# Placing matmul operands at different offsets modulo 256 bytes in SBUF, in a two-layer hybrid block kernel

## Chip, cores and metric

One core of a Trainium2 chip. The metric is the device time of one execution in microseconds; lower is better. All times stand for the whole program, from inputs in HBM to the output in HBM.

## What is computed

The reference runs two layers over 512 tokens of width 1024, all in float32:

```python
h = rms_norm(x, g_pre_mix)
proj = h @ w_in                                  # q, k, v, qi, ki, wi, xr, gr, zu, zv, gates
y_a = dsa_attention(q, k, v, qi, ki, wi)         # indexer picks 128 keys, then attention
y_b = rg_lru(conv(xr)) * gelu(gr)
y_c = chunked_spatial_gating(gelu(zu), rms_norm(gelu(zv)))
merged = einsum(sigmoid(gates), [y_a, y_b, y_c] @ w_branch)
x = x + rms_norm(merged @ w_out, g_post_mix)
f = square(relu(rms_norm(x) @ w_ffn_up)) @ w_ffn_down
x = x + rms_norm(f, g_post_ffn)
x = x + rms_norm((p @ w_ple) * sigmoid(x @ w_ple_gate), g_post_ple)
```

## The kernel before

Activations lie transposed: 128 features on the partitions, the 512 tokens along the free dimension, so one tile is 128 x 512 floats, 2 KB in each partition. A float32 product is made of three fast products (`mm3`, L296 to L299): every operand is split into a high part, rounded to the chip's `fp32r` type, and a low part, what is left; the matmuls are high by high, low weights by high activations, high weights by low activations. So TensorE gets three matmuls with 512 columns for each 128 x 128 block of weights, and each of them has weights of its own to load.

The names of the operands are those of the trace. `wr` is a weight tile as it comes by DMA (128 x 1024 floats, three buffers), `wh` and `wl` its two parts (four buffers each); `prep` (L231) issues the transfer on SyncE's queue, makes `wh` on ScalarE (L242) and `wl` on VectorE (L243), and `getw` (L246) keeps this three tiles ahead. `xh0` to `xh7` and `xl0` to `xl7` are the two parts of the normed activations ("the parts of x", `XS`, L470); they stream in the input projections, in the up projection of the feed-forward part and in its gate. `K0`, `K1`, `V0`, `V1` are 8 KB tiles that serve in turn as keys, values, merged activations and as the hidden activations of the even quarters of the feed-forward part (`K` the high parts, `V` the low ones); `A0` to `A7` (high) and `B0` to `B7` (low) hold the hidden activations of the odd quarters (L1064 to L1069), and before that queries, branch inputs and temporaries. In `ps<-xh,wl` the streamed operand stands first and the loaded one second.

The order of the work is written out by hand: `gemm` (L301) runs the blocks of one weight tile, 24 matmuls, into one of eight PSUM banks; `gemm_arriving` (L334, matmuls at L355) does the first four output tiles of a stage block by block while the activations are still being made; `gemm_halves` (L321) does the last three tiles of a stage in token halves of 256 columns. `tokens` (L578, L589) swaps the operands, so that x is loaded and weights stream. A planner with a clock of its own (`tick`, L285) puts indexer, attention and recurrence between these matmuls when the program is built; it knows no address.

Where a tile lies comes from the order in which the tags of a pool are first asked for: the pools `cp`, `wp`, `tp` and `ep` follow each other, and in each the tags follow each other with their buffers. In the kernel before, `lead` (L122) ends at a multiple of 256 bytes. All tiles after it are 2 KB, 4 KB or 8 KB, so each of x's parts, `K`, `V`, `A`, `B`, `M`, `R`, `wr`, `wh`, `wl` and `tmp` begins at a multiple of 256 bytes in its partition. Slices of them that are loaded or streamed are 512, 1024 or 2048 bytes apart, so every matmul of `mm3` has both operands at the same place modulo 256.

```python
76      def slot(tag, dt=F32, big=False):
77          return cp.tile([128, 4, S] if big else [128, S], dt, tag=tag, name=nm(tag))
...
122     cp.tile([128, LEAD // 4], F32, tag="lead", name="lead")
123     X = [cp.tile([128, S], F32, tag=f"X{k}", name=f"X{k}") for k in range(KT)]
...
240         hi = wp.tile([128, 1024], F32R, tag="wh", name=nm("wh"), bufs=NWB)
241         lo = wp.tile([128, 1024], F32R, tag="wl", name=nm("wl"), bufs=NWB)
242         A.copy(hi, raw)
243         V.tensor_sub(lo, raw, f32v(hi))
...
296     def mm3(ps, wh, wl, xh, xl, start, stop):
297         PE.matmul(ps, wh, xh, start=start, stop=False)
298         PE.matmul(ps, wl, xh, start=False, stop=False)
299         PE.matmul(ps, wh, xl, start=False, stop=stop)
...
470     XS = [(slot(f"xh{k}", F32R), slot(f"xl{k}", F32R)) for k in range(KT)]
```

Of the kernel before, what the change touches and what calls it, by code (L numbers as in the profile page):

```python
# [8 lines left out]
F32 = mybir.dt.float32  # L9
F32R = mybir.dt.float32r  # L10
# [40 lines left out]
def hybrid_block_kernel(ctx, tc, xT, pT, pos, vec, bsp, freq, w_in, w_tok, w_lru, w_sp, w_br, w_out, w_up, w_dn, w_ple, w_gate, out, depth=DEPTH, dbg=None):  # L51
    nc = tc.nc
    V, A, G, PE = nc.vector, nc.scalar, nc.gpsimd, nc.tensor

    cp = ctx.enter_context(tc.tile_pool(name="cp", bufs=1))
# [7 lines left out]
    def nm(p):  # L63
        uid[0] += 1
        return f"{p}_{uid[0]}"

    def tmp(dt=F32):
        return tp.tile([128, S], dt, tag="tmp", name=nm("tmp"), bufs=NTMP)
# [4 lines left out]
    def bank():  # L73
        return pp.tile([128, 512], F32, tag="ps", name=nm("ps"), bufs=8)

    def slot(tag, dt=F32, big=False):
        return cp.tile([128, 4, S] if big else [128, S], dt, tag=tag, name=nm(tag))
# [168 lines left out]
    def getw(key, ahead=LA):  # L246
        assert order[nget[0]][0] == key, (order[nget[0]][0], key)
        nget[0] += 1
        while nprep[0] < min(nget[0] + ahead, len(order)):
            prep()  # L250
        return prepared.pop(key)
# [49 lines left out]
    def gemm(ps, w, xs, kk, c0=0, st=None, r=FULL):  # L301

        h3, l3 = [v.rearrange("p (k c) -> p k c", k=kk) for v in w]
        for k in range(kk):
            if st is not None and k == kk - 2:
                st.partial()
            mm3(ps, h3[:, k, c0:c0 + 128], l3[:, k, c0:c0 + 128], xs[k][0][:, r], xs[k][1][:, r], k == 0, k == kk - 1)
            tick(0.65 * width(r) / S)
# [12 lines left out]
    def gemm_halves(keys, xs, evac, done):  # L321


        ws = [getw(key, LA if i == 0 else 0) for i, key in enumerate(keys)]
        for r in HALVES:
            for i, w in enumerate(ws):
                ps = bank()[:, :S // 2]
                gemm(ps, w, xs, KT, r=r)
                evac(i, r, ps)
                if r is HALVES[1] and nprep[0] < len(order):  # L330
                    prep()
            done(r)

    def gemm_arriving(keys, xs, source, ranges, arrived=None, lag=LAG, tail=TAIL):  # L334


        n = len(keys)
        ws = [getw(key, 0) for key in keys[:-1]]
        pss = [bank() for _ in keys]
        last = {}  # L340
        for r in ranges:
            gen = source(r)
            for k in range(KT):
                with ordered(last):
                    next(gen)
                    todo = [(o, k) for o in range(len(ws))]
                    if len(ws) < n and k == lag:
                        ws.append(getw(keys[-1], 0))
                        todo += [(n - 1, q) for q in range(k + 1)]
                    if r is ranges[-1] and k >= KT - tail:  # L350
                        todo = [] if k < KT - 1 else [(o, q) for o in range(n) for q in range(KT - tail, KT)]
                    for i, (o, q) in enumerate(todo):
                        h3, l3 = [v.rearrange("p (k c) -> p k c", k=KT) for v in ws[o]]
                        for m in range(3):
                            PE.matmul(pss[o][:, r], (h3, l3, h3)[m][:, q], xs[q][m // 2][:, r], start=q == 0 and m == 0, stop=q == KT - 1 and m == 2)  # L355
                        if r is ranges[-1] and q == KT - 1 and o < n - 1:
                            prep()
                tick(0.65 * len(todo) * width(r) / S)
            if arrived is not None:
                arrived(r)  # L360
        while nprep[0] < nget[0] + LA:
            prep()
        return pss
# [84 lines left out]
    class Norm:  # L448
# [16 lines left out]
        def source(self, r):  # L465
            while r.start not in self.gens:
                tick(0.1)
            return self.gens[r.start]

    XS = [(slot(f"xh{k}", F32R), slot(f"xl{k}", F32R)) for k in range(KT)]  # L470

    def x_tiles(r, xs, g=None, st=None, ys=None, bc=None, gp=None, on_g=()):

        def updated(d):
            if ys is not None and d < KT:
                if gp is None:
                    V.tensor_mul(ys[d][:, r], ys[d][:, r], bc)
                else:  # L480
                    V.scalar_tensor_tensor(ys[d][:, r], ys[d][:, r], gp[:, d:d + 1], bc, op0=ALU.mult, op1=ALU.mult)
                (G if d in on_g else V).tensor_add(X[d][:, r], X[d][:, r], ys[d][:, r])  # L482

        updated(0)
        for d in range(KT):
            x = X[d][:, r]
            if xs is not None:
                hi, lo = [v[:, r] for v in xs[d]]
                if g is None:
                    A.copy(hi, x)  # L490
                else:
                    A.activation(hi, x, AF.Copy, scale=g[:, d:d + 1])  # L492
                if st is not None:
                    st.square(x, r)
            updated(d + 1)
            if st is not None:
                st.accumulate(r)
            if xs is not None:
                if g is None:
                    V.tensor_sub(lo, x, f32v(hi))  # L500
                else:
                    V.scalar_tensor_tensor(lo, x, g[:, d:d + 1], f32v(hi), op0=ALU.mult, op1=ALU.subtract)  # L502
            yield d
# [28 lines left out]
    for l in range(depth):  # L532
# [6 lines left out]
        if l == 0:  # L539
            st = Stats()  # L540

            def gen():
                tiles = x_tiles(FULL, XS, vc[:, V_PRE:V_PRE + 8], st)
                for k in range(KT):
                    first_parts(k)
                    yield next(tiles)
# [5 lines left out]
        rt = st.rt  # L552
        first = gemm_arriving([("in", l, f"xr{j}") for j in range(3)], XS, norm.source if l else lambda r: gen0, HALVES if l else (FULL,), st.row(D, R), 0, TAIL if l else 1)

        def proj(name, ahead=LA):
            ps = bank()
            gemm(ps, getw(("in", l, name), ahead), XS, KT)
            return ps
# [11 lines left out]
        def rope(ps, n=128):  # L570
            t1, u = tmp(), tmp()
            V.tensor_mul(t1[:n], ps[:n], Cr[:n])
            V.stream_shuffle(u[:n], ps[:n], mask=SHUF)
            G.tensor_mul(u[:n], u[:n], Sr[:n])  # L574
            G.tensor_add(t1[:n], t1[:n], u[:n])  # L575
            return t1

        def tokens(n, fn):  # L578
# [3 lines left out]
            for t0 in (0, 2):  # L582
                pss = [bank(), bank()]
                for k in range(KT):
                    wh, wl = [v[:, k % 2] for v in ws[k // 2]]
                    for t, ps in enumerate(pss, t0):
                        xh, xl = [v[:, t * 128:(t + 1) * 128] for v in XS[k]]
                        for i, (x, w) in enumerate(((xh, wh), (xl, wh), (xh, wl))):
# [247 lines left out]
        for j in range(4):  # L836
# [7 lines left out]
            r, i = tmp(), tmp()  # L844
# [165 lines left out]
        for j in range(4):  # L1010
            f = rope(proj(f"q{j}"))
# [31 lines left out]
        def out_evac(d, r, ps):  # L1043
            st.add(ps, r)
            A.activation(Y[d][:, r], ps, AF.Copy, scale=col(V_POST + d))

        for d in range(5):
            ps = bank()
            gemm(ps, getw(("out", l, d)), M, KT)
            out_evac(d, FULL, ps)  # L1050
        norm = Norm(st, D, lambda r, bc: x_tiles(r, XS, vc[:, V_FFN:V_FFN + 8], st2, Y, bc, on_g=(1, 3, 5)))
        gemm_halves([("out", l, d) for d in (5, 6, 7)], M, lambda i, r, ps: out_evac(5 + i, r, ps), norm.complete)


        R = cp.tile([128, S], F32, tag="R", name=nm("R"))
        first = gemm_arriving([("up", l, 0, i) for i in range(4)], XS, norm.source, HALVES, st2.row(D, R))
        ps = bank()
# [172 lines left out]
```

## Time and profile before

| | |
|---|---|
| time, median of 3 runs | 1858.88 us (1858.13 to 1859.21) |
| the profiled execution: its own time | 1859.11 us |
| the profiled execution: its span | 1857.4 us |
| granted TensorE clock, mean | 0.99 of full speed |
| TensorE busy with matmuls | 1804.0 us (97%) |
| VectorE / ScalarE / GpSimd busy | 63% / 43% / 19% |
| read from HBM | 164 MB, 90 GB/s |

The span runs from the first to the last instruction of the profiled execution; its own time lies a little above it, and close to the median. PE is TensorE's matmul side, PEld its loading of weights, DVE VectorE, ACT ScalarE, POOL GpSimd, SPq the queue on which SyncE issues transfers. Matmuls are pipelined: the duration of one in the trace is longer than the distance from its start to the start of the next, and it is the distance that adds up.

### The profile page before, as it was taken

What the parts mean: (1) busy time and instruction counts of PE and PEld (TensorE: products, weight loads), DVE (VectorE), ACT (ScalarE), POOL (GpSimd) and SP (SyncE); (2) the same over time, 40 slices, a digit from 0 to 9 for tenths busy, and PEclk for the clock granted to TensorE, in tenths of its full rate; (3) what the DMA queues carried; (4) which work ended last, traced back from release to release, by engine and by line L of the source; (5) the groups of instructions that cost most, each with busy time, mean ns of one, the idle gap of its engine ahead of it and who ended that gap; (6) DMA issues with size and microseconds to landing.
All of it is one profiled execution on the core that took longest, in us unless ns stands there. A gap on an engine that the chain in (4) does not pass through costs nothing.

```text
span 1857.4 us, 22874 instructions
## 1 busy us (share of the span) xinstructions
PE 1804.0 (97%) x8798; PEld 1507.9 (81%) x8798; DVE 1161.0 (63%) x1939; ACT 800.9 (43%) x1292; POOL 361.3 (19%) x292
## 2 busy tenths in 40 slices
PE   8899999999999999999998999999999999999997
PEld 7787777888888888888887877877888888888886
DVE  6689986666386253533685999866563852545355
ACT  5466435564353231323554572455544432222233
POOL 3513212210140000003354141222003200000033
PEclk9999999999999999999999999999999999999998
DMA  5122222222223222232212122221222222222321
GB/s 172 63 91 90 87 97 84 76 78 82 80 91 103 100 93 102 91 114 91 89 60 97 66 93 92 102 80 69 91 80 91 91 91 102 92 101 94 111 80 58
DMA packets 49678, 167.77 MB, mean 90 GB/s; under 512 B 6048, under 2 KB 8864, under 8 KB 49568
## 3 DMA queue, kind: packets, MB, share of 16 engines
q1 hardware_dynamic: 47376, 163.64, 25.7%
q10 hardware_dynamic: 2192, 2.67, 0.4%
q8 instruction: 69, 1.13, 0.2%
q14 instruction: 41, 0.34, 0.1%
HBM read 164.19 MB, written 2.10 MB: 90 GB/s over the span
## 4 chain that ended last, share of the span: by engine, by line
PE 72%; DVE 14%; POOL 5%; issue 4%; ACT 4%; DMA 0%; SPq 0%; POOLq 0%; DVEq 0%; ACTq 0%
PE ps L297 20%; PE ps L299 20%; PE ps L298 20%; PE ps L589 4%; PE ps L355 4%; DVE wl L243 2%; DVE tmp L706 2%; DVE m L704 2%; POOL tmp L574 1%; POOL tmp L575 1%; PE ps L958 1%; POOL sacc L397 1%; POOL X L482 1%; PE ps L671 1%; DVE tmp L781 1%
## 5 line engine op out<-in xcount | busy, mean ns | idle before, releaser
L242 ACT CAST wh<-wr 128x1024 fp32r<-128x1024 f32 x303 | 316.7, 1049 | 453.2 <-PE ps L299 369.2
L243 DVE TENSOR_TENSOR wl<-wr,wh 128x1024 fp32r<-128x1024 f32 x303 | 386.0, 1278 | 190.7 <-ACT wh L242 189.9
L297 PE MATMUL ps<-xh,wh 128*128 128x512 f32 (+1 forms) x1296 | 502.2, 388 | 0.0
L298 PE MATMUL ps<-xh,wl 128*128 128x512 f32 (+1 forms) x1296 | 495.1, 382 | 3.0 <-DVE wl L243 3.0
L299 PE MATMUL ps<-xl,wh 128*128 128x512 f32 (+1 forms) x1296 | 495.4, 382 | 0.0
L397 POOL TENSOR_TENSOR sacc<-sacc,tmp 128x256 f32<-128x256 f32 (+1 forms) x99 | 109.7, 1109 | 893.7 <-issue 584.5
L299 PEld LDWEIGHTS ps<-xl,wh 128*128 128x128 f32 x1296 | 243.7, 188 | 48.2
L298 PEld LDWEIGHTS ps<-xh,wl 128*128 128x128 f32 x1296 | 244.0, 188 | 46.9 <-DVE wl L243 3.8
L297 PEld LDWEIGHTS ps<-xh,wh 128*128 128x128 f32 x1296 | 243.8, 188 | 45.5 <-issue 1.9
L299 PE MATMUL ps<-V,wh 128*128 128x512 f32 (+1 forms) x528 | 195.5, 370 | 0.0
L297 PE MATMUL ps<-K,wh 128*128 128x512 f32 (+1 forms) x432 | 158.2, 366 | 0.0
L298 PE MATMUL ps<-K,wl 128*128 128x512 f32 (+1 forms) x432 | 157.9, 365 | 0.0
L299 PE MATMUL ps<-B,wh 128*128 128x512 f32 x336 | 131.0, 390 | 0.0
L297 PE MATMUL ps<-A,wh 128*128 128x512 f32 x320 | 125.0, 391 | 0.0
L298 PE MATMUL ps<-A,wl 128*128 128x512 f32 x320 | 124.6, 389 | 0.0
L1089 DVE TENSOR_TENSOR M<-M,ps 128x512 f32<-128x512 f32 x48 | 33.0, 688 | 141.4 <-PE ps L299 141.4
L299 PEld LDWEIGHTS ps<-V,wh 128*128 128x128 f32 x528 | 99.5, 188 | 16.8
L1077 DVE TENSOR_TENSOR tmp<-ps,R 128x512 f32<-128x512 f32 x64 | 43.9, 691 | 108.4 <-PE ps L299 108.4
L355 PE MATMUL ps<-xl,wh 128*128 128x256 f32 (+1 forms) x264 | 88.2, 334 | 7.7 <-DVE xl L502 6.9
L297 PEld LDWEIGHTS ps<-K,wh 128*128 128x128 f32 x432 | 81.5, 189 | 13.2
L298 PEld LDWEIGHTS ps<-K,wl 128*128 128x128 f32 x432 | 81.5, 189 | 13.1
L355 PE MATMUL ps<-xh,wh 128*128 128x256 f32 (+1 forms) x264 | 86.5, 328 | 1.0 <-ACT xh L492 1.0
(237 smaller groups left out, 2738.5 us busy)
## 6 DMA issues: line engine op xcount, KB each, us to landing
wr<-in_w_in_dram SPq DMA_DIRECT2D x95, 512.0 KB, 3.2
wr<-in_w_up_dram SPq DMA_DIRECT2D x64, 512.0 KB, 3.2
wr<-in_w_dn_dram SPq DMA_DIRECT2D x64, 512.0 KB, 3.2
wr<-in_w_br_dram SPq DMA_DIRECT2D x24, 512.0 KB, 3.2
wr<-in_w_tok_dram SPq DMA_DIRECT2D x16, 512.0 KB, 3.2
wr<-in_w_out_dram SPq DMA_DIRECT2D x16, 512.0 KB, 3.2
wr<-in_w_gate_dram SPq DMA_DIRECT2D x16, 512.0 KB, 3.2
X<-in_xT_dram SPq DMA_DIRECT2D x8, 256.0 KB, 5.2
```

What stands on the lines that cost most here:

```text
L242: A.copy(hi, raw)
L243: V.tensor_sub(lo, raw, f32v(hi))
L297: PE.matmul(ps, wh, xh, start=start, stop=False)
L298: PE.matmul(ps, wl, xh, start=False, stop=False)
L299: PE.matmul(ps, wh, xl, start=False, stop=stop)
L355: PE.matmul(pss[o][:, r], (h3, l3, h3)[m][:, q], xs[q][m // 2][:, r], start=q == 0 and m == 0, stop=q == KT - 1 and m == 2)
L397: G.tensor_add(sacc[:, r], sacc[:, r], self.q[r.start, r.stop])
L589: PE.matmul(ps, x, w, start=k == 0 and i == 0, stop=k == KT - 1 and i == 2)
L704: V.max(m8, (sc if r == 0 else wk)[:, :n])
L706: V.match_replace(wk[:, :n], m8, (sc if r == 0 else wk)[:, :n], -3.0e38)
L1077: V.tensor_mul(t, ps, R)
L1089: V.tensor_add(F[d], F[d], ps)
```

## The change

Four filler tiles are put into the pool `cp`, ahead of the parts of x, between x and `K`/`V`, between these and `A`/`B`, and after them. So that the groups lie in that order, `K`, `V`, `A` and `B` are asked for once at this point, ahead of their first use. The fillers are 32, 32, 32 and 224 bytes in each partition. Modulo 256 the parts of x then begin at 32, `K` and `V` at 64, `A` and `B` at 96, and all that follows, `R`, `M`, `wr`, `wh`, `wl` and `tmp`, at 64 (320 bytes in all). X itself, the rope tables and `sacc` stay where they were. Nothing else is changed.

```diff
@@ -467,7 +467,23 @@
                 tick(0.1)
             return self.gens[r.start]
 
+
+    GAPS = (32, 32, 32, 224)
+
+    def gap(i):
+        if GAPS[i]:
+            cp.tile([128, GAPS[i] // 4], F32, tag=f"gap{i}", name=f"gap{i}")
+
+    gap(0)
     XS = [(slot(f"xh{k}", F32R), slot(f"xl{k}", F32R)) for k in range(KT)]
+    gap(1)
+    for n in ("K0", "K1", "V0", "V1"):
+        slot(n, F32R, True)
+    gap(2)
+    for n in range(8):
+        slot(f"A{n}", F32R)
+        slot(f"B{n}", F32R)
+    gap(3)
 
     def x_tiles(r, xs, g=None, st=None, ys=None, bc=None, gp=None, on_g=()):
```

## Rows read from the trace of the kernel before

**Rows 1.** The page: busy time by engine, and the chain that ended last.

```profile
PE 1804.0 (97%) x8798; PEld 1507.9 (81%) x8798; DVE 1161.0 (63%) x1939; ACT 800.9 (43%) x1292; POOL 361.3 (19%) x292
...
PE 72%; DVE 14%; POOL 5%; issue 4%; ACT 4%; DMA 0%; SPq 0%; POOLq 0%; DVEq 0%; ACTq 0%
PE ps L297 20%; PE ps L299 20%; PE ps L298 20%; PE ps L589 4%; PE ps L355 4%; DVE wl L243 2%; DVE tmp L706 2%; DVE m L704 2%; POOL tmp L574 1%; POOL tmp L575 1%; PE ps L958 1%; POOL sacc L397 1%; POOL X L482 1%; PE ps L671 1%; DVE tmp L781 1%
```

**Rows 2.** Timeline, PE, ends of three runs of 192 matmuls: start us, us, what.

```profile
606.75 0.39 PE L297 MATMUL ps<-K,wh 128*128 128x512 f32 x1
...
650.04 0.39 PE L299 MATMUL ps<-V,wh 128*128 128x512 f32 x1
650.27 0.39 PE L297 MATMUL ps<-xh,wh 128*128 128x512 f32 x1
...
693.56 0.39 PE L299 MATMUL ps<-xl,wh 128*128 128x512 f32 x1
693.79 0.39 PE L297 MATMUL ps<-A,wh 128*128 128x512 f32 x1
...
737.08 0.39 PE L299 MATMUL ps<-B,wh 128*128 128x512 f32 x1
```

**Rows 3.** Groups of the page and by form: xcount | busy us, mean ns | idle.

```profile
L297 PE MATMUL ps<-xh,wh 128*128 128x512 f32 (+1 forms) x1296 | 502.2, 388 | 0.0
...
L355 PE MATMUL ps<-xh,wh 128*128 128x256 f32 (+1 forms) x264 | 86.5, 328 | 1.0 <-ACT xh L492 1.0
...
L299 PE MATMUL ps<-B,wh 128*128 128x512 f32 x336 | 131.0, 390 | 0.0
...
L298 PE MATMUL ps<-A,wl 128*128 128x512 f32 x320 | 124.6, 389 | 0.0
...
L298 PE MATMUL ps<-B,wl 128*128 128x512 f32 x80 | 31.3, 391 | 0.0
...
L299 PE MATMUL ps<-A,wh 128*128 128x512 f32 x64 | 24.9, 389 | 0.0
```

**Rows 4.** Stretches at either clock (PEclk the share granted), and steps in the first.

```profile
999.43:1002.40 2.97, 2.97 (x8) 2.31 (x7) 2.94 (x5) 0.00 (x0) 1.00 (x1) 0.50 0.54 185
606.75:650.05 43.30, 43.30 (x193) 35.86 (x192) 11.70 (x11) 12.41 (x16) 0.00 (x0) 1.00 0.28 95
...
999.86 0.63 PE L589 MATMUL ps<-wh,xh 128*128 128x512 f32 x1
...
1001.14 0.63 PE L589 MATMUL ps<-wh,xh 128*128 128x512 f32 x1
```

**Rows 5.** Timeline, PE and PEld: a matmul, the next weights' load, the next matmul.

```profile
691.07 0.39 PE L297 MATMUL ps<-xh,wh 128*128 128x512 f32 x1
691.07 0.19 PEld L298 LDWEIGHTS ps<-xh,wl 128*128 128x128 f32 x1
...
691.30 0.39 PE L298 MATMUL ps<-xh,wl 128*128 128x512 f32 x1
```

**Rows 6.** The page: weight transfers (count, KB, us to landing), and VectorE's share of preparing.

```profile
L243 DVE TENSOR_TENSOR wl<-wr,wh 128x1024 fp32r<-128x1024 f32 x303 | 386.0, 1278 | 190.7 <-ACT wh L242 189.9
...
wr<-in_w_up_dram SPq DMA_DIRECT2D x64, 512.0 KB, 3.2
```

**Rows 7.** Groups by form, VectorE: two streams from SBUF, and one from PSUM.

```profile
L369 DVE TENSOR_TENSOR B<-tmp,A 128x512 fp32r<-128x512 f32 x32 | 21.9, 684 | 0.0
...
L369 DVE TENSOR_TENSOR tmp<-ps,tmp 128x512 fp32r<-128x512 f32 x16 | 11.0, 689 | 7.1 <-ACT tmp L368 4.6 <-POOL tmp L575 2.4
```

**Rows 8.** Timeline, PE, after an interruption: ends of nine steps.

```profile
544.14 0.40 PE L298 MATMUL ps<-xh,wl 128*128 128x512 f32 x1
...
546.22 0.39 PE L298 MATMUL ps<-xh,wl 128*128 128x512 f32 x1
```

**Rows 9.** Timeline, PE, 256 columns: ends of four steps and of 22 steps.

```profile
516.18 0.28 PE L355 MATMUL ps<-xh,wh 128*128 128x256 f32 x1
...
516.65 0.28 PE L355 MATMUL ps<-xh,wl 128*128 128x256 f32 x1
...
532.84 0.28 PE L355 MATMUL ps<-xh,wl 128*128 128x256 f32 x1
...
535.48 0.28 PE L355 MATMUL ps<-xl,wh 128*128 128x256 f32 x1
```

## Prediction

> **What bounds the kernel now.** I read the page first: TensorE is busy for 1804.0 of 1857.4 us and holds 72% of the chain that ended last, the three matmuls of `mm3` (L297 to L299) 20% each; VectorE follows with 14% [rows 1]. So the time is mostly the number of matmuls times the distance from the start of one to the start of the next. That distance comes from the timeline, over three unbroken runs of 192 matmuls of 512 columns (first and last row of each): with K and V streaming, 606.75 to 650.04; with the parts of x, 650.27 to 693.56; with A and B, 693.79 to 737.08 [rows 2]. Each is 43.29 us over 191 steps, 226.6 ns. The reader is to see that it is the same to the rounding in all three, and that in all three both operands lie at the same place modulo 256: the kernel before has no run that differs in the one thing that the change alters. How many matmuls are concerned comes from the groups: x streams in 3 groups of 1296 (L297 to L299) and 3 of 264 (L355), 4680; A and B stream in one group of 336, two of 320, two of 80 and one of 64, 1200 [rows 3]. Together 5880.
>
> What a matmul could cost is seen where the granted clock is at its lower level. At 999.43 to 1002.40 it is 0.50 (1.2 GHz); three steps take 1001.14 - 999.86 = 1.28 us, 426.7 ns each, and the window 606.75 to 650.05 has 1.00 (2.4 GHz) [rows 4]. Half of 426.7 is 213.3. So at full clock each matmul pays 226.6 - 213.3 = 13.3 ns over its columns, and at half clock nothing. The load of the next weights starts together with the matmul (both at 691.07) and ends at 691.26, before the next matmul at 691.30 [rows 5]: two reads run side by side through the first half of every matmul. A cost that is there at full rate and gone at half rate is what two colliding reads would look like; it is also what a fixed step that half rate hides would look like. That is the whole question.
>
> **The change, part by part.** (1) Four filler tiles: no instruction, no transfer; 320 bytes a partition. They cost nothing. (2) K, V, A and B are asked for once more, early: this settles only where they lie; no instruction, no wait, no queue is moved. (3) K, V, M, R, the weight buffers, `tmp`: all 64 bytes further. Weights against K and V stay at difference 0, so I leave those matmuls at 226.6 ns. (4) The weight transfers now land 64 bytes past a multiple of 256. The trace has no such landing. Now they take 3.2 us [rows 6], and a tile's 24 matmuls take 24 x 226.6 ns = 5.4 us, with three raw buffers ahead: half as long again would still hide behind the matmuls, so the sum takes 0; without that cover each late tile would cost the excess directly. (5) VectorE and ScalarE read and write at the new places. Two streams out of SBUF, `B<-tmp,A`, both at multiples of 256, take 684 ns for 512 columns; with one stream from PSUM, `tmp<-ps,tmp`, 689 ns [rows 7]. Equal places do not slow VectorE, so there is nothing to win or lose there: 0, within 5 ns a piece. (6) What is left: 4680 matmuls with x 32 bytes ahead of the weights, and 1200 with A or B 32 bytes behind.
>
> The price of (6) is not in the trace; it has to be bounded. Best end: the 13.3 ns go altogether, 5880 x 13.3 = 78 us, 1781. Worst end: after an interruption the steps stay long for a while, 544.14 to 546.22 for nine steps, 231.1 ns, 4.5 ns above the steady value [rows 8]; all 5880 at that level is 26 us, 1885. That the steps are longer there, with the same tiles at the same places, speaks for a cost that depends on how the two reads lie against each other. There are steps below the steady value as well: with 256 columns, 516.18 to 516.65 is four steps in 0.47 us (117 ns at most after the rounding of 0.01), where 532.84 to 535.48 is 22 steps at exactly 120.0 [rows 9]: 3 ns less. A shift of 32 bytes is 8 columns, 3.3 ns of the stream at 213.3 / 512 ns a column: a step of the same size as the differences in timing under which these steps vary.
>
> I take 2 ns less for each of the 5880, two thirds of the 3 ns that the rows show, because x and A/B are moved in opposite directions and the same effect need not help both. 5880 x 2 = 11.8 us. TensorE is idle for only 53 of 1857 us [rows 1], so nearly all of it reaches the end; after it the weight preparation still fits (1.28 us on VectorE for the 5.4 us of matmuls of a tile [rows 6]), so nothing new becomes late. The profiled execution took 1859.1 us (span 1857.4 and 1.7 around it), 0.2 over the median of 1858.9: 1859.1 - 11.8 = 1847.3, against the median **1847**.
>
> A rule that speaks against all this: the Trainium skill, page "TensorE: Matmul & The Clock Gate", section "Part 2: What happens when you issue a matmul", says that loading the next weights and streaming the present operand use two independent read ports and that the one takes no bandwidth from the other. By that the sum is 0 and the time stays at 1858.9. The same page's formula in "Back-to-back issue gap" gives, as an estimate for 512 columns, 215.8 ns; the trace here has 226.6, so something costs 10.8 ns more than the page knows, and the rule leaves it open what.
>
> **The rivals.** *No dependence on the place.* The 13.3 ns are a fixed step between two matmuls with weights of their own. For it: the same 226.6 in all three runs, the same 13.3 at 256 columns (120.0 - 106.7), VectorE's indifference to places, and that two streams of different pace pass each other as often wherever they start. Against it: the steps that vary between 117 and 120, and between 226.6 and 231. Time: 1858.9. The rule of the skill named above ends here too.
>
> *The shift makes x worse.* The load begins within 0.01 us of its matmul. If it begins about 3.3 ns behind, x, now 32 bytes (3.3 ns) behind the weights' place, stands exactly at that place when the load starts, and both read the same lines at once; A and B move away from it. Then 4680 matmuls go to 231.1 ns, +4.5 x 4680 = 21 us, and A/B win 2 x 1200 = 2.4: 1858.9 + 18.7 = 1877.5. For it: x is four fifths of the affected matmuls, so its sign decides; with a 3.7 us bound, 0.8 ns more per x matmul is enough. Against it: at 10 ns resolution the lead of the matmul is not seen, and the long steps of rows 8 come after interruptions only and die out.
>
> *The whole excess goes* (the best end above): 1781 if complete for both, 1797 for x alone. Against it: no step of 512 columns in the rows is anywhere near 213.3.
>
> **How the numbers follow.** A difference under 0.2% (3.7 us) can't be told from no change here. Shorter steps for x and A/B, little or much: 0.46, mostly near 1847, with a tail to the best end; no dependence: 0.30; x worse: 0.24. The range runs from 1805 (9 ns of the 13.3 gone) to 1885 (all 5880 at the long level); about 0.05 lies below and 0.08 above. The likeliest case's own range is 1805 to 1855. Faster by over 0.2%: 0.46, within: 0.30, slower: 0.24.
>
> **What would show it.** The three runs of rows 2, timed again: x and A/B near 224.6 ns and K/V at 226.6 bears the forecast out; all three at 226.6 is the first rival; x near 231 and A/B below 226.6 the second. At half clock the step must stay 426.7 whatever happens. The landing of a weight tile should stay near 3.2 us, VectorE's and ScalarE's means as they are. The forecast is wrong if the time moves while the x runs keep 226.6 (then it came from waits, not from reads), or if K/V, whose difference is unchanged, moves as much as x.

## The result, and the profile after

The changed kernel takes 1878.67 us in the median of four runs (1875.80 to 1880.23) against 1858.51 of before: a ratio of 1.0107, interval 1.0089 to 1.0124. It is 20 us slower. The profiled execution is the 1875.80 one.

The page of the changed kernel: span, busy time by engine, the chain by engine, and the landing of a weight tile.

```profile
span 1874.1 us, 22874 instructions
...
PE 1829.7 (98%) x8798; PEld 1503.3 (80%) x8798; DVE 1160.8 (62%) x1939; ACT 801.7 (43%) x1292; POOL 362.4 (19%) x292
...
PE 72%; DVE 14%; POOL 5%; ACT 4%; issue 4%; DMA 0%; SPq 0%; POOLq 0%; ACTq 0%; DVEq 0%
...
wr<-in_w_up_dram SPq DMA_DIRECT2D x64, 512.0 KB, 3.3
```

Against [rows 1] the instructions are the same in number, VectorE, ScalarE and GpSimd do the same work to within 1.1 us each, and the chain is shared out in the same way. Only TensorE has grown, by 25.7 us, while the span grew by 16.7: its idle time fell from 53.4 to 44.4 us.

The timeline of the changed kernel, PE, at the ends of the three runs of 192 matmuls (start us, us, what):

```profile
606.55 0.39 PE L297 MATMUL ps<-K,wh 128*128 128x512 f32 x1
...
649.87 0.39 PE L299 MATMUL ps<-V,wh 128*128 128x512 f32 x1
650.10 0.40 PE L297 MATMUL ps<-xh,wh 128*128 128x512 f32 x1
...
694.66 0.40 PE L299 MATMUL ps<-xl,wh 128*128 128x512 f32 x1
694.90 0.40 PE L297 MATMUL ps<-A,wh 128*128 128x512 f32 x1
...
739.46 0.39 PE L299 MATMUL ps<-B,wh 128*128 128x512 f32 x1
```

These answer to [rows 2]. K/V, whose difference to the weights is still 0: 43.32 us over 191 steps, 226.8 ns, 0.03 us in all over before. x: 44.56 us, 233.3 ns. A/B: 44.56 us, 233.3 ns. Both shifts cost 6.7 ns a matmul, ahead or behind alike. From the first row to the last it takes 132.91 us where [rows 2] have 130.33: 2.58 us more, and 384 matmuls by 6.7 ns are 2.57. In this stretch the loss reaches the time one to one.

Two more stretches of the changed kernel's timeline, PE: 92 steps of 256 columns with x streaming, and three steps at half clock, with the window that shows the clock (the last column but two).

```profile
914.14 0.28 PE L297 MATMUL ps<-xh,wh 128*128 128x256 f32 x1
...
925.02 0.28 PE L299 MATMUL ps<-xl,wh 128*128 128x256 f32 x1
```

```profile
1003.30:1009.90 6.60, 5.69 (x13) 4.46 (x14) 4.67 (x7) 1.38 (x2) 2.78 (x2) 0.50 0.53 149
...
1004.80 0.63 PE L605 MATMUL ps<-wh,xh 128*128 128x512 f32 x1
...
1006.08 0.63 PE L605 MATMUL ps<-wh,xh 128*128 128x512 f32 x1
```

With 256 columns the shift helps: 10.88 us over 92 steps, 118.3 ns, where [rows 9] have 120.0. And at half clock it does nothing: 1.28 us for three steps, as in [rows 4].

In `tokens` the weights stream and x is loaded, so there, too, the two now lie 32 bytes apart. The ends of one run of 26 of its matmuls, before and in the changed kernel:

```profile
230.04 0.39 PE L589 MATMUL ps<-wh,xh 128*128 128x512 f32 x1
235.71 0.39 PE L589 MATMUL ps<-wh,xl 128*128 128x512 f32 x1
...
228.59 0.39 PE L605 MATMUL ps<-wh,xh 128*128 128x512 f32 x1
234.42 0.40 PE L605 MATMUL ps<-wh,xl 128*128 128x512 f32 x1
```

5.67 us over 25 steps against 5.83: 226.8 ns and 233.2. These matmuls lose as much as the others.

Who waited for whom (us in total, times, longest), entries of PE on the preparation of weights and of x, before and in the changed kernel:

```profile
PE ps L589 <- DVE wl L243: 16.3, 6, 4.2
PE ps L355 <- DVE xl L502: 6.9, 8, 3.7
PE ps L298 <- DVE wl L243: 6.3, 4, 1.6
...
PE ps L605 <- DVE wl L243: 14.0, 6, 4.2
PE ps L355 <- DVE xl L518: 6.1, 10, 2.5
PE ps L298 <- DVE wl L243: 3.1, 4, 1.2
```

TensorE waits most for these preparations on VectorE. When its matmuls get longer, the waits get shorter (for `wl` 17.1 us instead of 22.6), and that part of the loss never reaches the end.

### The profile page after: what moved, and what is told of

It reads as the page before. It is cut to its first block, busy times and chain, and to the rows that moved or that the text cites. A ratio compares the mean times of both kernels' runs of the same rounds, so it can differ in the third digit from the quotient of the medians.

```text
span 1874.1 us, 22874 instructions
## 1 busy us (share of the span) xinstructions
PE 1829.7 (98%) x8798; PEld 1503.3 (80%) x8798; DVE 1160.8 (62%) x1939; ACT 801.7 (43%) x1292; POOL 362.4 (19%) x292
## 4 chain that ended last, share of the span: by engine, by line
PE 72%; DVE 14%; POOL 5%; ACT 4%; issue 4%; DMA 0%; SPq 0%; POOLq 0%; ACTq 0%; DVEq 0%
PE ps L297 20%; PE ps L299 20%; PE ps L298 20%; PE ps L605 4%; PE ps L355 4%; DVE wl L243 2%; DVE tmp L722 2%; DVE m L720 2%; POOL tmp L590 1%; POOL tmp L591 1%; PE ps L974 1%; POOL sacc L397 1%; POOL X L498 1%; PE ps L687 1%; DVE tmp L797 1%
## 5 line engine op out<-in xcount | busy, mean ns | idle before, releaser
L297 PE MATMUL ps<-xh,wh 128*128 128x512 f32 (+1 forms) x1296 | 508.1, 392 | 0.0
L298 PE MATMUL ps<-xh,wl 128*128 128x512 f32 (+1 forms) x1296 | 501.6, 387 | 0.7 <-DVE wl L243 0.7
L299 PE MATMUL ps<-xl,wh 128*128 128x512 f32 (+1 forms) x1296 | 501.4, 387 | 0.0
L298 PEld LDWEIGHTS ps<-K,wl 128*128 128x128 f32 x432 | 81.5, 189 | 13.3
```

## The experiments

The question: what makes a step 233.3 ns instead of 226.7? The place of each operand by itself, the difference between the two, or something else that the new order of tiles brings along? Unless a diff says otherwise, a kernel here is the changed one with other fillers. All steps below are worked out as above, from the first and the last row of the runs of 192 matmuls.

**All at 32 past a multiple of 256.**

```diff
-    GAPS = (32, 32, 32, 224)
+    GAPS = (32, 0, 0, 0)
```

> One filler of 32 bytes ahead of the parts of x and none after it: x, K, V, A, B and the weights all begin at 32 modulo 256, so the difference between streamed and loaded operand is 0 everywhere. If the difference decides: the runs of 192 matmuls with x, K/V and A/B all step in 226.7 ns, and the time is that of before, 1858.5 us within 4. If what decides is that an operand does not begin at a multiple of 64 bytes: all three runs step in 233.3 ns, K/V too, and the time is some 1880 to 1890.

1859.34 us against 1859.40, ratio 1.000, interval 0.9990 to 1.0009. x and A/B in its timeline:

```profile
647.67 0.39 PE L297 MATMUL ps<-xh,wh 128*128 128x512 f32 x1
...
690.96 0.39 PE L299 MATMUL ps<-xl,wh 128*128 128x512 f32 x1
691.19 0.39 PE L297 MATMUL ps<-A,wh 128*128 128x512 f32 x1
...
734.48 0.39 PE L299 MATMUL ps<-B,wh 128*128 128x512 f32 x1
```

43.29 us over 191 steps each, 226.6 ns. The new order of the tiles, the early asking for K, V, A and B, and starting off a multiple of 64 cost nothing. With the differences back at 0, the whole loss is gone.

**x alone, A and B alone.**

```diff
-    GAPS = (32, 32, 32, 224)
+    GAPS = (0, 32, 0, 0)
```

> One filler of 32 bytes after the parts of x: x at 0, all else at 32 modulo 256. Only x differs from the weights, by 32 bytes ahead. If the difference decides: x steps in 233.3 ns, K/V and A/B in 226.7, and x's four fifths of the loss come back alone: 1858.5 plus 16, about 1874. If absolute places off a multiple of 64 decide: x (at 0) 226.7, K/V and A/B (at 32) 233.3, and a time of 1862 to 1870.

1870.45 us against 1859.40, ratio 1.0059, interval 1.0044 to 1.0074. The three runs:

```profile
607.10 0.40 PE L297 MATMUL ps<-K,wh 128*128 128x512 f32 x1
...
650.40 0.39 PE L299 MATMUL ps<-V,wh 128*128 128x512 f32 x1
650.63 0.40 PE L297 MATMUL ps<-xh,wh 128*128 128x512 f32 x1
...
695.19 0.40 PE L299 MATMUL ps<-xl,wh 128*128 128x512 f32 x1
695.43 0.39 PE L297 MATMUL ps<-A,wh 128*128 128x512 f32 x1
...
738.75 0.39 PE L299 MATMUL ps<-B,wh 128*128 128x512 f32 x1
```

x, the only one that stands at 0, is the slow one: 233.3 ns, while K/V and A/B at 32 take 226.7 and 226.8. The difference decides. Of the 16 us that were expected from x alone, 11 came.

```diff
-    GAPS = (32, 32, 32, 224)
+    GAPS = (0, 0, 32, 224)
```

> Fillers of 32 bytes ahead of A/B and 224 after them: A and B at 32, all else at 0. Both theories expect 233.3 ns in the A/B runs and 226.7 in the x and K/V runs; 1200 matmuls by 6.7 ns are 8 us at most, so 1862 to 1867. If the losses of x alone and of A/B alone do not add up to the 20 us of the change, the two are not independent.

1865.91 us against 1859.40, ratio 1.0033, interval 1.0022 to 1.0043; A/B 233.4 ns, x and K/V 226.6. The two parts add up to 17.6 us, the change to 20.2; by their intervals the parts make 12 to 22. They are independent as far as this can be told.

**Larger differences.** In the first kernel x lies 64 ahead of the weights, K/V 64 behind, A/B 128 behind; in the second x 96 ahead, K/V 96 behind, A/B level; in the third K/V lie 256 behind and A/B 288.

```diff
-    GAPS = (32, 32, 32, 224)
+    GAPS = (0, 128, 64, 128)
```

> Fillers 0, 128, 64, 128: x at 0, K/V at 128, A/B at 192, weights at 64 modulo 256. Every operand is at a multiple of 64 bytes; x lies 64 ahead of the weights, K/V 64 behind, A/B 128 behind. If absolute places off a multiple of 64 decide: 226.7 ns in all three runs and 1858.5 us. If the difference decides: at least one of the three leaves 226.7; a collision of the two reads that is worst at a distance of 32 and gone at a large one would give steps below 226.7 somewhere, down to 216; one in which 0 is the best place gives 227 to 240 in all three.

1877.09 us against 1859.40, ratio 1.0096, interval 1.0081 to 1.0111. Its three runs:

```profile
609.38 0.39 PE L297 MATMUL ps<-K,wh 128*128 128x512 f32 x1
...
653.09 0.39 PE L299 MATMUL ps<-V,wh 128*128 128x512 f32 x1
653.33 0.39 PE L297 MATMUL ps<-xh,wh 128*128 128x512 f32 x1
...
697.88 0.39 PE L299 MATMUL ps<-xl,wh 128*128 128x512 f32 x1
698.11 0.39 PE L297 MATMUL ps<-A,wh 128*128 128x512 f32 x1
...
742.50 0.39 PE L299 MATMUL ps<-B,wh 128*128 128x512 f32 x1
```

228.8 ns for K/V, 233.2 for x, 232.4 for A/B: all longer than at 0, none shorter, though every operand stands at a multiple of 64.

```diff
-    GAPS = (32, 32, 32, 224)
+    GAPS = (0, 192, 160, 0)
```

> Fillers 0, 192, 160, 0: x 96 bytes ahead of the weights, K/V 96 behind, A/B and the weights at the same place (96 past a multiple of 256). By the theory that the difference decides and 0 is the best place: A/B 226.7 ns, x and K/V between 228 and 236. By a theory of two reads that collide when near: x and K/V at or below 226.7, as far apart as they are. Time 1862 to 1885 by the first, under 1862 by the second.

1880.9 us (one run; before beside it 1859.4). x 234.2 ns, K/V 233.4, A/B 226.7: as expected if 0 is the best place, and not if it is nearness that costs.

```diff
-    GAPS = (32, 32, 32, 224)
+    GAPS = (0, 256, 32, 224)
```

> Fillers 0, 256, 32, 224: x and weights at 0 modulo 512, K/V 256 behind them modulo 512, A/B 288 behind. If the pattern repeats every 256 bytes: K/V 226.7 ns and A/B 233.3, as at 0 and at 32 behind. If its period is 512 or more: K/V leaves 226.7, or A/B leaves 233.3. x 226.7 either way. Time near 1866 by the first.

1864.1 us (one run; before beside it 1859.4). K/V and A/B:

```profile
604.71 0.39 PE L297 MATMUL ps<-K,wh 128*128 128x512 f32 x1
...
648.01 0.39 PE L299 MATMUL ps<-V,wh 128*128 128x512 f32 x1
...
691.75 0.40 PE L297 MATMUL ps<-A,wh 128*128 128x512 f32 x1
...
736.32 0.40 PE L299 MATMUL ps<-B,wh 128*128 128x512 f32 x1
```

226.7 ns at 256 as at 0, 233.4 at 288 as at 32: at these two places the pattern repeats after 256 bytes.

**Differences below 32.** The parts of x are slices of one tile here, begun 16, 4 and 8 bytes in (made from the kernel before, all else at 0):

```diff
-    XS = [(slot(f"xh{k}", F32R), slot(f"xl{k}", F32R)) for k in range(KT)]
+    XT = cp.tile([128, 2 * KT * S + 8], F32R, tag="xs", name="xs")
+    XP = [XT[:, 4 + i * S:4 + (i + 1) * S] for i in range(2 * KT)]
+    XS = [(XP[2 * k], XP[2 * k + 1]) for k in range(KT)]
+    cp.tile([128, 56], F32, tag="gap", name="gap")
```

> The parts of x in one tile, begun 16 bytes in, so that x lies at 16 modulo 256 and all else at 0: x 16 bytes behind the weights. If what matters is being in the same 32-byte piece: 226.7 ns in the x runs and 1858.5 us. If any difference counts, down to pieces of 16 bytes or less: x steps in 229 to 236 ns and the time is 1864 to 1876.

> The same with x begun one float (4 bytes) in: x 4 bytes behind the weights. If whole pieces of 16 or 32 bytes are read: the x runs keep about 226.7 ns unless a read off a multiple of 16 bytes costs something of its own. If the difference counts to the byte: 229 to 236 ns, as at 32.

> x in one tile begun two floats (8 bytes) in. At 16 bytes the x runs stepped in 231.6 ns, at 4 bytes in 238.3. If being off a multiple of 16 bytes adds a cost of its own, 8 bytes is near 238; if only being off a multiple of 8 does, near 231.6. If 226.7 is to be beaten at a small difference at all, it would have to show here.

16 bytes (4 floats, as in the diff): 231.6 ns and 1865.7 us. 4 bytes (1 in place of the 4): 238.3 ns and 1888.3 us. 8 bytes (2 in place of the first 4; the slices are then two columns longer than what is used): 233.3 ns and 1872.5 us. Each is one run, with before at 1857.7, 1857.7 and a median of 1858.3. Being in the same piece of 16 or 32 bytes does not help; one float off is the worst of all:

```profile
658.09 0.40 PE L297 MATMUL ps<-xs,wh 128*128 128x512 f32 x1
...
703.60 0.40 PE L299 MATMUL ps<-xs,wh 128*128 128x512 f32 x1
```

At 4 bytes the step lies above the 229 to 236 ns that were expected, and at 8 bytes it is near neither 238 nor 231.6. In these three kernels x alone, of the operands of `mm3`, stands off a multiple of 32 bytes, so whether its place costs something of its own, beside the difference, is not separated. No run has x in one tile begun at 0, so it is the steps that count here, and not the times.

The third column is from runs of 93 matmuls with 256 columns (92 steps) in the same traces.

| streamed less loaded operand, bytes modulo 256 | step at 512 columns, ns | step at 256 columns, ns | from |
|---|---|---|---|
| -96 | 234.2 | 117.3 | x, second kernel of the larger differences |
| -64 | 233.2 | 117.8 | x, first of them |
| -32 | 233.3 | 118.3 | x, the change |
| **0** | **226.6 to 226.8** | 119.9 | before; all at 32; K/V of the change; 256 |
| 4, 8, 16 | 238.3, 233.3, 231.6 | 123.0, 119.9, 113.5 | x in one tile |
| 32 | 233.3 | no run | A/B, the change |
| 64 | 228.8 | 117.8 | K/V, first of the larger differences |
| 96 | 233.4 | 119.9 | K/V, second of them |
| 128 | 232.4 | no run | A/B, first of them |

With 512 columns, 0 is the best of the differences tried, and no kernel here is faster than the one before by more than the noise. With 256 columns it is not: there the lowest step is the one at 16 bytes. Its run, and the same run before:

```profile
910.78 0.28 PE L297 MATMUL ps<-xs,wh 128*128 128x256 f32 x1
921.22 0.28 PE L299 MATMUL ps<-xs,wh 128*128 128x256 f32 x1
...
908.47 0.28 PE L297 MATMUL ps<-xh,wh 128*128 128x256 f32 x1
919.50 0.28 PE L299 MATMUL ps<-xl,wh 128*128 128x256 f32 x1
```

10.44 us against 11.03. At 4 bytes the step is longer at both widths.

**Only the loads of wl.** A filler of 32 bytes between the buffers of `wh` and `wl` (in the kernel before, L512 to L513; `tmp`, which follows, moves along):

```diff
         hi = wp.tile([128, 1024], F32R, tag="wh", name=nm("wh"), bufs=NWB)
+        if not chunks:
+            wp.tile([128, 8], F32, tag="gapw", name="gapw")
         lo = wp.tile([128, 1024], F32R, tag="wl", name=nm("wl"), bufs=NWB)
```

> A filler of 32 bytes between the buffers of wh and wl: wl (and what follows it, tmp) at 32 modulo 256, all else at 0. wl is loaded while the matmul of L297 streams, and used by the matmul of L298. If two reads side by side decide: the step from L297 to the next matmul grows and those from L298 and L299 stay near 226.7. If a matmul's own two operands decide: the step from L298 grows. If neither, all three change. A third of the loads are concerned, so 3 to 10 us over before.

1883.5 us (one run; before beside it 1857.7), far more than expected. Its timeline, x streaming:

```profile
655.40 0.40 PE L297 MATMUL ps<-xh,wh 128*128 128x512 f32 x1
655.64 0.39 PE L298 MATMUL ps<-xh,wl 128*128 128x512 f32 x1
655.87 0.40 PE L299 MATMUL ps<-xl,wh 128*128 128x512 f32 x1
656.10 0.40 PE L297 MATMUL ps<-xh,wh 128*128 128x512 f32 x1
```

Steps of 0.24, 0.23 and 0.23, and 0.70 us for every three, 233.3 ns each on average. The longest begins with the matmul beside which `wl` is loaded, which speaks for reads side by side. But the two others, 0.46 us together and 230 ns each, are longer than 226.7 as well, so all three change. Three matmuls lose as much in all as if each of the three loads had been moved. So a matmul does not simply pay for the pair of reads that it overlaps.

**One odd tile among sixteen.** Only `xl7` is moved (made from the kernel before):

```diff
-    XS = [(slot(f"xh{k}", F32R), slot(f"xl{k}", F32R)) for k in range(KT)]
+    XS = []
+    for k in range(KT):
+        xh = slot(f"xh{k}", F32R)
+        if k == KT - 1:
+            cp.tile([128, 8], F32, tag="gap0", name="gap0")
+        XS.append((xh, slot(f"xl{k}", F32R)))
+    cp.tile([128, 56], F32, tag="gap1", name="gap1")
```

> Only the last low part, xl7, is moved: 32 bytes behind all the rest, which stands at 0 modulo 256. One matmul in 24 of a tile streams it. If each matmul pays for its own pair of reads: one step in 24 grows by some 7 to 13 ns, the x runs average 226.9 to 227.2 ns, and the time stays within 3 us of before. If one odd pair throws the whole stream out of its even pace, and it needs some ten steps to find it again as after an interruption: about ten steps in 24 are long, the x runs average 228.5 to 230 ns, and the time is 6 to 14 us over before.

Its timeline, PE: the odd matmul of one tile at 656.68, and that of the next at 662.17.

```profile
656.68 0.40 PE L299 MATMUL ps<-xl,wh 128*128 128x512 f32 x1
656.92 0.39 PE L297 MATMUL ps<-xh,wh 128*128 128x512 f32 x1
...
659.00 0.39 PE L297 MATMUL ps<-xh,wh 128*128 128x512 f32 x1
...
662.17 0.40 PE L299 MATMUL ps<-xl,wh 128*128 128x512 f32 x1
```

From the odd matmul on ten steps take 2.32 us, 232.0 ns each; the fourteen after them take 3.17 us, 226.4. Then the next odd one comes. Nine of those ten matmuls have both operands level. It is the same picture as after an interruption in [rows 8]: there nine steps take 2.08 us, and the nine from 656.92 on take 2.08 here. One odd pair throws the stream out of its pace, and it takes ten steps to find it again: the second expectation holds for the steps (228.6 ns over the run, 645.98 to 689.64). Its time does not follow: 1858.3 us against 1859.4, and not 6 to 14 us more. But that one execution had a mean granted clock of 0.993, and the one beside it 0.990.

> The kernel with xl7 alone moved once more, timed in rounds: its x runs stepped in 228.6 ns, yet its one time, 1858.3, lay no higher than before, with 27 us at half clock in its profile where before has 41. If the longer steps count and the clock hid them: 1.3 ns on some 3750 matmuls, 5 us less what waits absorb, 1861 to 1864 in the median. If the time is really unmoved: within 1 us of before.

1860.02 us against 1858.30, ratio 1.0012, interval 1.0003 to 1.0021: a loss of 1.7 us, which lies between the two expectations. The steps are again 228.6. The 1.3 ns that were expected are too few: 228.6 less 226.7 is 1.9, which over x's 3864 matmuls of 512 columns makes 7 us. Part of these the granted clock gave back: it was 0.991 to 0.994 in the eleven runs, 0.9923 on average, and 0.990 to 0.992 in the fifteen of before, 0.9908 on average. As an estimate, 0.0015 of 1858 us are 2.8 us. Why the clock is higher here, no run shows.

## Why the prediction was wrong

**The sign of the one term.** The step that failed is "I take 2 ns less for each of the 5880". It measured 6.7 ns more for the matmuls of 512 columns. I took the sign from [rows 9], four steps of 256 columns that were shorter than the steady ones, and carried it to 512 columns. Even there the 3 ns were less sure than stated: 0.47 us between starts rounded to 0.01 is 115 to 120 ns a step, not 117 at most. At 256 columns the gain does exist: 118.3 against 120.0 ns. But only 816 of x's 4680 matmuls have 256 columns, which is 1.4 us. For 512 columns the only rows off the steady pace were [rows 8], and they were longer; the forecast should have been priced from them.

**What the count left out.** Part (6) has 5880 matmuls. The 384 of `tokens`, where x is the loaded operand, are missing from it: their difference went from 0 to 32 bytes too, and they stepped in 233.2 ns instead of 226.8.

**What the steady 226.6 was.** I asked whether the 13.3 ns over the columns were a collision to be got rid of or a fixed step. The rows allowed a third reading, and it is the one that the runs show: 226.6 is the pace that the stream settles into when streamed and loaded operand lie level, and the lowest pace found at 512 columns. [Rows 8] already showed it being lost and found again. What the 13.3 ns themselves are stays open.

**The rivals.** The second, "the shift makes x worse", had the time, 1877.5 against 1878.7, and x's sign. Its mechanism was wrong in half: A/B were to win and lose as much per matmul as x, so it is not a matter of which read runs ahead. Its price, 231.1 ns, was too low for x (233.3). That its time came out is luck: too low a price and a gain that did not come were made up for by a loss that did not all reach the end. "No dependence" is refuted at 512 columns by all the kernels with a difference other than 0. The rule of the Trainium skill that ended there too ("TensorE: Matmul & The Clock Gate", "Part 2: What happens when you issue a matmul") is that loading the next weights takes no SBUF read bandwidth from the running matmul; by it the step would have stayed. The trace disagrees: with the same instructions the step goes from 226.7 to 233.3 by the difference of the two addresses alone. Whether it is bandwidth that is lost, or something else between the two reads, no run shows.

**"Nearly all of it reaches the end".** This was wrong as well. By the measured steps 3864 matmuls of 512 columns with x and 1200 with A/B, 6.7 ns each, are 33.9 us; less the 1.4 us at 256 columns, 32.5; with the 384 of `tokens`, at most 2.6 us more, 35. The median rose by 20.2. In the stretch of [rows 2] the loss counted in full (2.58 of 2.57 us). So what was absorbed was absorbed elsewhere, above all where TensorE waits for other engines: in the profiled execution its idle time fell by 9.0 us. A further part is the clock: the mean granted clock of this execution is 0.993, before 0.990, and the other three runs of the change, at 0.990 to 0.992, took 1878.6 to 1880.2. As an estimate, 0.003 of 1874 us are 5.6 us. The kernel with A and B alone shows a similar size: its two runs at 0.993 took 1861.2 and 1862.0 us, its seven at 0.990 and 0.991 took 1865.0 to 1866.7. In the profiled execution 35 less 9.0 and 5.6 leaves 20.4 us, and the span grew by 16.7; the rest is not accounted for.

**The parts costed at nothing** were right: order, fillers and early asking (all at 32: ratio 1.000), and VectorE and ScalarE (busy times within 1 us). The weight transfers landed in 3.3 us in place of 3.2. That isn't the new place: in the kernels with the weights back at 0, A and B alone among them, it is 3.3 too.

**The range** held the result, the chance for "slower" was 0.24. The sign of the forecast was wrong, and that the range held is luck too: its upper end stood for 4.5 ns a matmul, and the 35 us of the measured steps, had they all reached the end, would have given some 1893. (Its lower end, 9 ns off each of 5880, is 1806 and not 1805.)

## What to carry to other kernels

Where every matmul loads weights of its own and streams 512 columns in this element type, keep the streamed and the loaded operand at the same place modulo 256 bytes: one odd tile in sixteen already spoils ten matmuls in 24 (1.7 us in all here), and one of the two weight parts spoils all. Fillers and new tiles ahead of such operands should therefore be multiples of 256 bytes, and after any change in the allocation the start-to-start distance in a long unbroken run tells in one look whether the pace is still there. With 256 columns the same rule does not hold: the step was shorter than at 0 at five of the eight differences tried. No kernel here was built to use that. A longer matmul costs its full price only where TensorE never waits; elsewhere part of it is paid by the waits.

## What the runs showed of the hardware that was not expected

- At 512 columns the step depends on the difference of the two addresses modulo 256, not on either address: 226.6 ns with all at 32 past a multiple, 233.3 with x at a multiple and the rest at 32.
- It is not a cost per pair. One odd matmul leaves ten long steps behind it (232.0 ns), and a third of the loads odd cost as much as all. Why a stream with level operands has an even pace that others lack is not shown by these runs.
- The sign depends on the number of columns: 32 bytes ahead, 512 columns lose 6.7 ns and 256 columns win 1.7. With 16 bytes, 512 columns lose 5.0 and 256 columns win 6.4 (113.5 against 119.9). At half clock the 6.7 ns do not show: 512 columns take 426.7 ns with the operands level and with them 32 apart.
